# Two output blocks of the branch merge begun in four other PSUM banks, attention's half first

## The chip, the cores and the metric

The kernel runs on one core of a Trainium2 chip. The metric is the device time of one execution in microseconds. Before the change three runs took 825.71, 826.19 and 828.87 us, a median of 826.19 us.

A core works with five engines that each take their own instructions strictly in the order in which they were written down: TensorE (PE, with its weight loads shown as PEld), VectorE (DVE), ScalarE (ACT), GpSimd (POOL) and SyncE (SP), which here only issues DMAs. An instruction that waits holds up all that stand behind it on its engine. Matmuls write to PSUM, which has eight banks of 128 x 512 float32; everything else lies in SBUF.

## The reference

The program is one layer of a trunk with two parallel branches over 512 tokens (and 16 meta tokens ahead of them) of width 1024. A combined projection of the normed input feeds an RWKV-7 recurrence, a forgetting attention ("FoX") and 2 x 1024 gates. The change concerns the line that merges the two branches:

```python
u = rmsnorm(h, norm_mix[l])
proj = u @ w_in[l]
...
gates = jax.nn.sigmoid((proj[..., C_RW + C_FX:] + b_gate[l]).astype(jnp.float32))
y_rw = rwkv7_branch(feat_rw, ...)
y_fx = fox_branch(feat_fx, b_f[l], q_gain[l], k_gain[l])
merged = gates[..., :D_MODEL] * (y_rw @ w_out_rw[l]) + gates[..., D_MODEL:] * (y_fx @ w_out_fx[l])
h = h + (merged @ w_o[l]).astype(h.dtype)
z = rmsnorm(h, norm_mlp[l])
h = h + (jnp.square(jax.nn.relu(z @ w_up[l])) @ w_down[l]).astype(h.dtype)
```

## The kernel before

Activations lie transposed, features on the partitions and tokens along the free dimension. Every float32 product is made of three matmuls of rounded parts: each operand is split into a high part (a copy by ACT to the type float32r) and a low part (the difference, by DVE), and `passes` gives the pairs high-high, high-low and low-high.

**The front** (up to about 400 us) is one interleaved program. Generators ("streams": the recurrence, attention, its features, the splitting of finished branch outputs, and at the lowest rank `projections`) each yield the model time at which they can go on, and `Turns.run` always lets the stream of lowest rank that is ready write its next matmuls. That fixes the order of PE; the order of the other engines is set by a scheduler of the language, from priorities and a model of its own. The last stream to have work is `projections`: 40 blocks of 128 output columns, of which the last 16 are the gates. For each it fetches the weights (SP), splits them (L550 on ACT, L551 on DVE), multiplies (L582) and empties the bank with `gate_job` (L595 on ACT, then L596, a DMA of the gate block from tile `gt` to memory `gd`, issued on ACT's queue).

PSUM is one pool for the whole kernel: four banks with the tag "sm" for everything small, two with "pj", one "ch" and one "py". The chain of the recurrence uses "ch" and "py" while it runs; the projections use "pj", and the other two when the chain is over.

**The merge** (L1250 to L1273) follows. It makes `merged` in eight blocks `m` of 128 features. For each block the weights `wout[m]` are loaded in two halves by `load_w`: the first half (k 0 to 3) belongs to the recurrence, the second (k 4 to 7) to attention. Raw halves, high parts `whi` and low parts `wlo` have rings of four buffers each, that is two blocks. For each of the two branches the block takes a gate tile `gl` from memory (L1261), a tanh on ACT (L1262), a bank "sm" by `ppo` and 12 matmuls (4 k's of 3 passes, L1267), which DVE takes out together with the gate (L1269). POOL adds the two branches (L1271), ACT and DVE split the sum into `mhi` and `mlo` (L1272, L1273). The split branch outputs `ys[k]` are the streaming operands, k 0 to 3 of the recurrence (k 0, 1 from its first two head pairs, ready early, and k 2, 3 from the last two) and k 4 to 7 of attention. After the merge come the product with `wo` (L1298, L1329), which takes its banks from both sets, and the MLP.

A tile ring gives its oldest buffer to a new tile, so a new `whi` waits until PE has finished with the `whi` four tiles before it.

Of the kernel before, what the change touches and what calls it, by code (L numbers as in the profile page):

```python
# [147 lines left out]
class Event:  # L148
    done = False
# [40 lines left out]
def kernel(ctx, tc, ht, x, win, par, cst, gain, lora, wout, wo, wup, wdn, out, dbg=None):  # L190
    nc = tc.nc
    dbg = dbg or {}
    mm = nc.tensor.matmul
# [89 lines left out]
    ps = ctx.enter_context(tc.tile_pool(name="ps", bufs=2, space=PSUM))  # L283
    gates_d = [dr.tile([128, S], F32, name=f"gd{i}") for i in range(16)]
    ys = {}
    quarters = [[wdn[i][256 * c:256 * c + 256] for c in range(8)] for i in range(4)]

    with ExitStack() as st:
# [254 lines left out]
        def convert(job, raws):  # L543
# [9 lines left out]
                w.append((hi, lo))  # L553
            return job, w

        def projections(total):
            fetched, done = None, 0
            while done < total:
                if fetched is None:
                    yield lambda: 0.0 if jobs else math.inf  # L560
                    fetched = fetch(jobs.pop(0))
                cur = convert(*fetched)
                fetched = fetch(jobs.pop(0)) if jobs else None
                while cur is not None:
                    (_, _, _, begin, parts, ev, need), w = cur
                    nxt = convert(*fetched) if fetched else None
                    fetched = fetch(jobs.pop(0)) if jobs else None
                    if need is not None:
                        yield need
                    evac = begin()  # L570
                    for a0, a1 in parts:
                        po = None
                        n = 0
                        for k in range(KB):
                            if k % 2 == 0 or a1 - a0 > 300:
                                yield lambda f=po is None: max(ck.ready(*w[k // 4]), block_bank()[0] if f else 0.0)
                            if po is None:
                                tag = block_bank()[2]
                                po = ppj(tag)[:, :a1 - a0]
                                lent.extend([tag] * (tag != "pj"))  # L580
                            for a, b in passes(wk(w, k), U):
                                mm(po, a, b[:, k, a0:a1], start=n == 0, stop=n == 23)  # L582
                                n += 1
                        evac(po, slice(a0, a1))
                        if tag in lent:
                            lent.remove(tag)
                    ev.done = True
                    done += 1
                    cur = nxt

        def gate_job(i):
            def begin():
# [13 lines left out]
        def two(j, k):  # L606
            ys[4 * j + k] = t = kp.tile([128, 2, S], F32R, name="ys", tag=SLOTS[(4 * j + k) // 2], bufs=2)
            return t[:, 0, :], t[:, 1, :]

        def divided():  # L610
            yield chained[1]
            for k in range(2):
                split(*two(0, k), y_rw[:, k, :])
            for k in range(3):
                yield fox_done[k]
                split(*two(1, k), y_fx[:, k, :])
            yield normalised[1][1]
            for k in range(2, 4):
                split(*two(0, k), y_rw[:, k, :])

        forgot = Event()

# [102 lines left out]
        def attention():  # L725
# [3 lines left out]
            for p in range(4):  # L729
# [67 lines left out]
                def mixed():  # L797

                    yield lambda: max(ck.ready(vt, vm, pTm, *pT), banks(1))
                    py = psm("py")  # L800
                    for e, hs in enumerate(hss):
                        mm(py[hs], vm[32 * e:32 * e + 16, hs], pTm[32 * e:32 * e + 16, :], start=True, stop=False)
                    for j, at in enumerate((0, 4, 8, 7)):
                        for e, hs in enumerate(hss):
                            mm(py[hs, 128 * j:], vt[:, j, hs], pT[e][:, at:at + 4 - j, :].rearrange("p a b -> p (a b)"), start=False, stop=j == 3)  # L805
                        if j == 0:
                            yield lambda: 0.0
                    if p < 3:
                        A.copy(y_fx[:, p, :], py)
                    else:  # L810
                        yield chained[1]
                        split(*two(1, 3), py)

                pes = yield from scored(0)
                for i in range(4):
# [411 lines left out]
        turns.add(3, fox_features())  # L1227
        turns.add(4, divided())
        turns.add(8, projections(24 + 16))
        for i in range(16):  # L1230
            ask(9, B_GATE + i, gate_job(i), SEQ)
        with tc.manual_schedule(engines={mybir.EngineType.PE}):
# [16 lines left out]

    with ExitStack() as st:  # L1250
        mp = st.enter_context(tc.tile_pool(name="mp", bufs=1))
        ahead = [load_w(wout[0])]
        mhi = mp.tile([128, KB, S], F32R, name="mhi")
        mlo = mp.tile([128, KB, S], F32R, name="mlo")
        table["pin"] = None
        for m in range(KB):
            w = ahead.pop() if ahead else load_w(wout[m])
            pp = []
            for br in range(2):
                g = mp.tile([128, S], F32, name=f"gl{br}", bufs=2)  # L1260
                nc.sync.dma_start(g, gates_d[8 * br + m])  # L1261
                act(g, g, AF.Tanh, scale=0.5)  # L1262
                po = ppo()
                n = 0
                for k in range(4 * br, 4 * br + 4):
                    for a, b in passes(wk(w, k), (0, 1)):
                        mm(po, a, ys[k][:, b, :], start=n == 0, stop=n == 11)  # L1267
                        n += 1
# [347 lines left out]
```

## Time and profile before

| | |
|---|---|
| median of three runs | 826.19 us (825.71 to 828.87) |
| the profiled execution's own time | 826.71 us |
| its span | 824.9 us, so 1.8 us lie around it |
| PE busy | 808.1 us (98%) |
| DVE, ACT, POOL busy | 607.8, 452.5, 120.0 us |
| matmuls of the merge (L1267) | 192, first at 400.1 us, last at 444.7 us |
| granted TensorE clock, mean over the core | 0.998 |

The chain of waits follows the work that ended last back from the end. The table of windows gives what each engine was busy in a stretch of time, and the timeline gives the instructions of one engine with their starts, durations and, in brackets, the idle time ahead of them and what ended it. Matmuls overlap in the array, so their starts are to be compared rather than their durations. PEclk is the share of full clock that TensorE was granted.

### The profile page before, as it was taken

Reading aid. Unit: us, or ns where it says so; the run is one execution under the profiler, and the core shown is the slowest. Engines: PE = TensorE matmul, PEld = TensorE weight load, DVE = VectorE, ACT = ScalarE, POOL = GpSimd, SP = SyncE. Lnnn points to the kernel's source line nnn. Section 1 sums busy time; section 2 is a strip of 40 time slices with the busy share of each in tenths; the row PEclk is TensorE's granted clock in tenths of the full one; section 3 lists DMA queues with packets and bytes.
Section 4 is the critical chain, followed back from the end, with each engine's and each line's share of the span. In section 5 each row is a group of like instructions: output and inputs, shape, how many; then the busy total and the mean of one; then the engine's idle time right before and its main releaser. Section 6 shows DMA issues by size and latency. Waiting matters only on the chain.

```text
span 824.9 us, 15506 instructions
## 1 busy us (share of the span) xinstructions
PE 808.1 (98%) x5886; PEld 667.3 (81%) x5886; DVE 607.8 (74%) x1196; ACT 452.5 (55%) x941; POOL 120.0 (15%) x124
## 2 busy tenths in 40 slices
PE   8999999998999999999999999999999999999998
PEld 6979887876987886778788889888888888888886
DVE  6797985687779855975267655875698678867988
ACT  7767548766575457664366534664445434543452
POOL 1021000010011000000022003100740174017400
PEclk9999999999999999999999999999999999999999
DMA  7222221211211311223687404533742365236532
GB/s 240 75 71 79 69 92 56 79 40 65 79 52 54 128 46 61 90 66 116 218 289 226 159 0 151 176 82 100 225 150 87 115 221 150 77 118 208 156 107 76
DMA packets 51483, 95.88 MB, mean 116 GB/s; under 512 B 5832, under 2 KB 7240, under 8 KB 51408
## 3 DMA queue, kind: packets, MB, share of 16 engines
q1 hardware_dynamic: 47680, 86.37, 33.0%
q0 software_dynamic: 1280, 4.20, 1.7%
q10 hardware_dynamic: 2448, 4.33, 1.5%
q8 instruction: 46, 0.75, 0.4%
q14 instruction: 29, 0.24, 0.1%
HBM read 88.56 MB, written 6.31 MB: 115 GB/s over the span
## 4 chain that ended last, share of the span: by engine, by line
PE 86%; DVE 5%; ACT 5%; issue 2%; DMA 1%; POOL 0%; DVEq 0%; ACTq 0%; SPq 0%
PE pj L582 22%; PE po L1357 21%; PE po L1484 12%; PE pd L1484 5%; PE po L1267 4%; PE po L1329 3%; PE pj L394 1%; PE pd L1298 1%; PE po L1298 1%; PE psc L751 1%; PE py L805 1%; PE psr L964 1%; PE ppt L788 1%; DVE wlo L551 1%; PE pch L1115 1%
## 5 line engine op out<-in xcount | busy, mean ns | idle before, releaser
L582 PE MATMUL pj<-uhi,whi 128*128 128x264 f32 (+1 forms) x480 | 164.3, 342 | 0.0
L582 PE MATMUL pj<-uhi,wlo 128*128 128x264 f32 (+1 forms) x480 | 153.9, 321 | 1.8 <-DVE wlo L551 1.8
L582 PE MATMUL pj<-ulo,whi 128*128 128x264 f32 (+1 forms) x480 | 153.8, 320 | 0.0
L242 DVE TENSOR_TENSOR wlo<-wraw,whi 128x512 fp32r<-128x512 f32 x84 | 81.0, 973 | 36.8 <-ACT whi L242 36.8
L582 PEld LDWEIGHTS pj<-uhi,whi 128*128 128x128 f32 x480 | 90.7, 189 | 12.9 <-issue 4.4
L582 PEld LDWEIGHTS pj<-uhi,wlo 128*128 128x128 f32 x480 | 90.7, 189 | 8.8 <-DVE wlo L551 2.2
L582 PEld LDWEIGHTS pj<-ulo,whi 128*128 128x128 f32 x480 | 91.0, 190 | 6.7 <-issue 1.6
L1357 PE MATMUL po<-zhi,whi 128*128 128x512 f32 (+1 forms) x248 | 94.8, 382 | 0.0
L1357 PE MATMUL po<-zlo,whi 128*128 128x512 f32 (+1 forms) x248 | 94.8, 382 | 0.0
L1357 PE MATMUL po<-zhi,wlo 128*128 128x512 f32 (+1 forms) x248 | 94.8, 382 | 0.0
L242 ACT CAST whi<-wraw 128x512 fp32r<-128x512 f32 x84 | 51.4, 617 | 53.5 <-PE po L1357 20.3
L551 DVE TENSOR_TENSOR wlo<-wraw,whi 128x512 fp32r<-128x512 f32 x78 | 53.8, 699 | 23.5 <-ACT whi L550 22.6
L550 ACT CAST whi<-wraw 128x512 fp32r<-128x512 f32 x78 | 47.7, 617 | 42.4 <-PE pj L582 41.7
L276 ACT CAST whi<-t 128x512 fp32r<-128x512 f32 x64 | 39.9, 624 | 44.6 <-DVE wlo L276 27.2
L1406 POOL TENSOR_TENSOR t<-traw 128x512 f32<-128x512 f32 x24 | 38.4, 1622 | 173.6 <-DMA traw<-in_wdn 173.6
L1484 PE MATMUL po<-wlo,fhi 128*128 128x512 f32 (+1 forms) x164 | 63.4, 387 | 0.2
L1484 PE MATMUL po<-whi,flo 128*128 128x512 f32 (+1 forms) x164 | 62.8, 384 | 0.0
L1484 PE MATMUL po<-whi,fhi 128*128 128x512 f32 (+1 forms) x164 | 62.3, 384 | 0.0
L276 DVE TENSOR_TENSOR wlo<-t,whi 128x512 fp32r<-128x512 f32 x64 | 43.5, 689 | 24.3 <-ACT whi L276 24.0
L1373 ACT CAST fhi<-R 128x768 fp32r<-128x768 f32 (+1 forms) x32 | 30.2, 945 | 49.1 <-DVE R L1380 26.1
L1357 PEld LDWEIGHTS po<-zlo,whi 128*128 128x128 f32 x248 | 46.6, 188 | 9.1
L1357 PEld LDWEIGHTS po<-zhi,wlo 128*128 128x128 f32 x248 | 46.6, 188 | 9.0
(330 smaller groups left out, 1706.4 us busy)
## 6 DMA issues: line engine op xcount, KB each, us to landing
wraw<-in_win SPq DMA_DIRECT2D x84, 256.0 KB, 2.6
wraw<-in_wup SPq DMA_DIRECT2D x60, 256.0 KB, 3.1
wraw<-in_wdn SPq DMA_DIRECT2D x48, 256.0 KB, 2.7
traw<-in_wdn SPq DMA_DIRECT2D x48, 256.0 KB, 3.5
gd<-gt ACTq DMA_DIRECT2D x16, 256.0 KB, 2.2
wraw<-in_wout SPq DMA_DIRECT2D x16, 256.0 KB, 3.9
gl<-gd SPq DMA_DIRECT2D x16, 256.0 KB, 3.8
traw<-in_wdn POOLq DMA_DIRECT2D x16, 256.0 KB, 3.1
```

The costliest lines, as they stand in the source:

```text
L242: casts.append((A.copy(hi, raw), low.tensor_tensor(lo, raw, hi.bitcast(F32), ALU.subtract)))
L276: return A.copy(hi, x), V.tensor_tensor(lo, x, hi.bitcast(F32), ALU.subtract)
L550: after(A.copy(hi, raw), last["ACT"])
L551: low[0] = V.tensor_tensor(lo, raw, hi.bitcast(F32), ALU.subtract)
L582: mm(po, a, b[:, k, a0:a1], start=n == 0, stop=n == 23)
L1267: mm(po, a, ys[k][:, b, :], start=n == 0, stop=n == 11)
L1298: mm(pd[i], a[:, k, 128 * i:128 * i + 128], b, start=k == 0 and n == 0, stop=k == 7 and n == 2)
L1329: mm(po, a[:, k, 128 * i:128 * i + 128], b[:, k, :], start=n == 0, stop=n == 23)
L1357: mm(po[:, t0:t1], a, b[:, k, t0:t1], start=n == 0, stop=n == 23)
L1373: A.copy(fhi[:, j, a:b], R[:, a:b])
L1406: eng.tensor_tensor(t, sums[c, pair] if c in (T1, T2) else c, d, ALU.add)
L1484: mm(x[i][:, cols], a[:, k, left, 128 * rows:128 * rows + 128], c[:, cols], start=start and k == 0 and n == 0, stop=stop and k == n_pairs ...
```

## The change

A new stream `merging`, of the rank of `projections`, begins when all projections are written down. For the blocks m = 0 and 1 it takes a bank of the other set for each branch (both "pj" banks for m = 0, "ch" and "py" for m = 1) and writes into it 6 matmuls of the recurrence's half (k 0 and 1) and all 12 of attention's half (k 4 to 7). Together these are 36 matmuls. The bank and the number of matmuls done are kept in `under`. The merge loop then takes these banks over, writes the missing 6 matmuls of the recurrence's half (k 2 and 3) for each of the two blocks, and goes on with blocks 2 to 7 in the banks "sm" as before. In all eight blocks attention's half (`br` 1) now comes first, so the sum is gathered in attention's gate tile. The weights of `wout[0]` are asked for inside the front.

```diff
--- before.py
+++ after.py
@@ -283,6 +283,7 @@
     ps = ctx.enter_context(tc.tile_pool(name="ps", bufs=2, space=PSUM))
     gates_d = [dr.tile([128, S], F32, name=f"gd{i}") for i in range(16)]
     ys = {}
+    under = {}
     quarters = [[wdn[i][256 * c:256 * c + 256] for c in range(8)] for i in range(4)]
 
     with ExitStack() as st:
@@ -553,6 +554,8 @@
                 w.append((hi, lo))
             return job, w
 
+        begun, parted, projected = [], {}, Event()
+
         def projections(total):
             fetched, done = None, 0
             while done < total:
@@ -564,6 +567,8 @@
                 while cur is not None:
                     (_, _, _, begin, parts, ev, need), w = cur
                     nxt = convert(*fetched) if fetched else None
+                    if done == total - 1:
+                        begun.append(load_w(wout[0]))
                     fetched = fetch(jobs.pop(0)) if jobs else None
                     if need is not None:
                         yield need
@@ -587,6 +592,31 @@
                     ev.done = True
                     done += 1
                     cur = nxt
+            projected.done = True
+
+        def merging():
+
+            yield projected
+            for m in range(2):
+                w = begun.pop() if m == 0 else load_w(wout[m])
+                pos = []
+                for br, ks in ((0, (0, 1)), (1, (4, 5, 6, 7))):
+                    if m:
+                        yield chained[1]
+                    tag = ("pj", ("ch", "py")[br])[m]
+                    yield lambda: max(ck.ready(*w[br]), ck.ring(tag, 1, 1 if m else 2))
+                    po = ppj(tag)
+                    n = 0
+                    for k in ks:
+                        while k not in parted:
+                            yield lambda: math.inf if k not in parted else 0.0
+                        yield lambda: ck.ready(parted[k])
+                        for a, b in passes(wk(w, k), (0, 1)):
+                            mm(po, a, ys[k][:, b, :], start=n == 0, stop=n == 11)
+                            n += 1
+                    pos.append((po, n))
+                under[m] = w, pos
+            return
 
         def gate_job(i):
             def begin():
@@ -607,16 +637,21 @@
             ys[4 * j + k] = t = kp.tile([128, 2, S], F32R, name="ys", tag=SLOTS[(4 * j + k) // 2], bufs=2)
             return t[:, 0, :], t[:, 1, :]
 
+        def part(j, k, y):
+            hi, lo = two(j, k)
+            split(hi, lo, y)
+            parted[4 * j + k] = lo
+
         def divided():
             yield chained[1]
             for k in range(2):
-                split(*two(0, k), y_rw[:, k, :])
+                part(0, k, y_rw[:, k, :])
             for k in range(3):
                 yield fox_done[k]
-                split(*two(1, k), y_fx[:, k, :])
+                part(1, k, y_fx[:, k, :])
             yield normalised[1][1]
             for k in range(2, 4):
-                split(*two(0, k), y_rw[:, k, :])
+                part(0, k, y_rw[:, k, :])
 
         forgot = Event()
 
@@ -809,7 +844,7 @@
                         A.copy(y_fx[:, p, :], py)
                     else:
                         yield chained[1]
-                        split(*two(1, 3), py)
+                        part(1, 3, py)
 
                 pes = yield from scored(0)
                 for i in range(4):
@@ -1227,6 +1262,7 @@
         turns.add(3, fox_features())
         turns.add(4, divided())
         turns.add(8, projections(24 + 16))
+        turns.add(8, merging())
         for i in range(16):
             ask(9, B_GATE + i, gate_job(i), SEQ)
         with tc.manual_schedule(engines={mybir.EngineType.PE}):
@@ -1249,20 +1285,18 @@
 
     with ExitStack() as st:
         mp = st.enter_context(tc.tile_pool(name="mp", bufs=1))
-        ahead = [load_w(wout[0])]
         mhi = mp.tile([128, KB, S], F32R, name="mhi")
         mlo = mp.tile([128, KB, S], F32R, name="mlo")
         table["pin"] = None
         for m in range(KB):
-            w = ahead.pop() if ahead else load_w(wout[m])
+            w, pos = under.get(m) or (load_w(wout[m]), [])
             pp = []
-            for br in range(2):
+            for br in (1, 0):
                 g = mp.tile([128, S], F32, name=f"gl{br}", bufs=2)
                 nc.sync.dma_start(g, gates_d[8 * br + m])
                 act(g, g, AF.Tanh, scale=0.5)
-                po = ppo()
-                n = 0
-                for k in range(4 * br, 4 * br + 4):
+                po, n = pos[br] if pos else (ppo(), 0)
+                for k in range(4 * br + n // 3, 4 * br + 4):
                     for a, b in passes(wk(w, k), (0, 1)):
                         mm(po, a, ys[k][:, b, :], start=n == 0, stop=n == 11)
                         n += 1
```

The number of matmuls stays the same, and up to the last projection all engines have the same rows in the same order. In the rows below the names are tiles with their numbers: `whi_5490` and `whi_5496` (with `wlo_5491`, `wlo_5497`) are the two halves of the weights of block m = 2 in both programs, the recurrence's and attention's; line numbers of the changed program are 30 to 35 higher.

ScalarE, from the last gate's bank on, before:

```order
L595 ACTIVATE gt_5374<-pj_5349,pr_64 128x512
L596 DMA gd15_95<-gt_5374 128x512
L242 CAST whi_5490<-wraw_5488 128x512
L242 CAST whi_5496<-wraw_5494 128x512
L1262 ACT_TABLE_LOAD
L1262 ACTIVATE gl0_5402<-gl0_5402 128x512
L1262 ACTIVATE gl1_5419<-gl1_5419 128x512
L1262 ACTIVATE gl0_5451<-gl0_5451 128x512
L1262 ACTIVATE gl1_5468<-gl1_5468 128x512
L242 CAST whi_5539<-wraw_5537 128x512
L1272 ACTIVATE mhi_5400<-gl0_5402 128x512
```

ScalarE at the same place in the changed program:

```order
L625 ACTIVATE gt_5386<-pj_5361,pr_64 128x512
L626 DMA gd15_95<-gt_5386 128x512
L242 CAST whi_5490<-wraw_5488 128x512
L1297 ACT_TABLE_LOAD
L1297 ACTIVATE gl1_5454<-gl1_5454 128x512
L1297 ACTIVATE gl0_5458<-gl0_5458 128x512
L1297 ACTIVATE gl1_5471<-gl1_5471 128x512
L1297 ACTIVATE gl0_5475<-gl0_5475 128x512
L242 CAST whi_5496<-wraw_5494 128x512
L242 CAST whi_5539<-wraw_5537 128x512
L1306 ACTIVATE mhi_5452<-gl1_5454 128x512
```

`whi_5490` still stands ahead of the load of the tanh table and the four tanhs of the gate tiles of m = 0 and 1, `whi_5496` has moved behind all four. `whi_5490` takes the buffer of the first half of m = 0 (`whi_5351` in the changed program, `whi_5390` before), `whi_5496` that of its second half.

VectorE, from the low parts of the same weights on, before:

```order
L242 TENSOR_TENSOR wlo_5491<-wraw_5488,whi_5490 128x512
L242 TENSOR_TENSOR wlo_5497<-wraw_5494,whi_5496 128x512
L1269 SCALAR_TENSOR_TENSOR gl0_5402<-gl0_5402,po_5405 128x512
L1269 SCALAR_TENSOR_TENSOR gl1_5419<-gl1_5419,po_5422 128x512
L1269 SCALAR_TENSOR_TENSOR gl0_5451<-gl0_5451,po_5454 128x512
L242 TENSOR_TENSOR wlo_5540<-wraw_5537,whi_5539 128x512
L1273 SCALAR_TENSOR_TENSOR mlo_5401<-gl0_5402,mhi_5400 128x512
```

VectorE at the same place in the changed program:

```order
L242 TENSOR_TENSOR wlo_5491<-wraw_5488,whi_5490 128x512
L1303 SCALAR_TENSOR_TENSOR gl1_5454<-gl1_5454,pj_5396 128x512
L1303 SCALAR_TENSOR_TENSOR gl0_5458<-gl0_5458,pj_5389 128x512
L1303 SCALAR_TENSOR_TENSOR gl1_5471<-gl1_5471,pj_5428 128x512
L242 TENSOR_TENSOR wlo_5497<-wraw_5494,whi_5496 128x512
L1303 SCALAR_TENSOR_TENSOR gl0_5475<-gl0_5475,pj_5421 128x512
L1307 SCALAR_TENSOR_TENSOR mlo_5453<-gl1_5454,mhi_5452 128x512
L242 TENSOR_TENSOR wlo_5540<-wraw_5537,whi_5539 128x512
```

`wlo_5497` stands behind three gates' products now, where it stood ahead of all of them.

TensorE in the changed program, from the last matmuls of m = 0 on (rows with x2 are two matmuls):

```order
L1301 MATMUL pj_5389<-ys_5298,whi_5351 128x512 x2
L1301 MATMUL pj_5389<-ys_5298,wlo_5352 128x512
L1301 MATMUL pj_5421<-ys_5295,whi_5411 128x512 x2
L1301 MATMUL pj_5421<-ys_5295,wlo_5412 128x512
L1301 MATMUL pj_5421<-ys_5298,whi_5411 128x512 x2
L1301 MATMUL pj_5421<-ys_5298,wlo_5412 128x512
L1301 MATMUL po_5503<-ys_5124,whi_5496 128x512 x2
L1301 MATMUL po_5520<-ys_5118,whi_5490 128x512 x2
L1301 MATMUL po_5503<-ys_5124,wlo_5497 128x512
```

TensorE before, around the same 49th matmul after the last projection:

```order
L1267 MATMUL po_5471<-ys_5115,whi_5447 128x512 x2
L1267 MATMUL po_5471<-ys_5115,wlo_5448 128x512
L1267 MATMUL po_5503<-ys_5118,whi_5490 128x512 x2
L1267 MATMUL po_5503<-ys_5118,wlo_5491 128x512
L1267 MATMUL po_5503<-ys_5121,whi_5490 128x512 x2
```

The last use of m = 0's first half is now in the 14th pair of rows (matmuls 40 to 42 after the last projection); before it was in the fourth (matmuls 10 to 12). The 49th matmul reads `whi_5496` and a bank "sm" that nobody holds; before, it read `whi_5490` and a bank that the first gate's product has to free.

## The prediction

> **What bounds the kernel now.** I read the page first: PE is busy for nearly the whole span and carries most of the chain of waits. So a PE instruction that starts later moves the end, and idle time elsewhere does not.
>
> ```profile
> span 824.9 us, 15506 instructions
> PE 808.1 (98%) x5886; PEld 667.3 (81%) x5886; DVE 607.8 (74%) x1196; ACT 452.5 (55%) x941; POOL 120.0 (15%) x124
> PE 86%; DVE 5%; ACT 5%; issue 2%; DMA 1%; POOL 0%; DVEq 0%; ACTq 0%; SPq 0%
> ```
>
> Next came the windows around the place of the change (columns: stretch, length, busy time of each engine, PEclk, DMA share, GB/s).
>
> ```profile
> 390.00:400.00 10.00, 10.00 (x46) 8.29 (x45) 4.19 (x7) 4.07 (x7) 0.00 (x0) 1.00 0.43 139
> 400.00:445.00 45.00, 43.97 (x194) 36.08 (x194) 25.71 (x39) 25.12 (x42) 9.55 (x7) 1.00 0.81 262
> 445.00:480.00 35.00, 35.00 (x160) 29.07 (x159) 21.21 (x37) 18.56 (x39) 2.09 (x2) 1.00 0.46 150
> ```
>
> The projections' last stretch and the stage behind the merge have no idle PE at all. The merge has 1.0 us. That bounds what the change can win: the matmuls are the same, and 36 of them only change their bank. PE's timeline shows where the microsecond lies.
>
> ```profile
> 400.06 0.62 PE L1267 MATMUL po<-ys,whi 128*128 128x512 f32 x2
> 408.90 0.62 PE L1267 MATMUL po<-ys,whi 128*128 128x512 f32 x2
> 410.72 0.39 PE L1267 MATMUL po<-ys,wlo 128*128 128x512 f32 x1
> 412.13 0.73 PE L1267 MATMUL po<-ys,whi 128*128 128x512 f32 x2 [1.03 <-DVE gl L1269]
> 444.90 0.39 PE L1298 MATMUL po<-whi,mhi 128*128 128x512 f32 x1
> ```
>
> Matmuls 1 and 48 of the merge start at 400.06 and 410.72, so one takes 10.66 / 47 = 0.227 us. The 49th could start at 410.95 and starts at 412.13, 1.18 us late: it needs a fifth bank "sm", and the first is freed by DVE only after the gate has come. The chain says why the gate is late.
>
> ```profile
> 401.28 5.43 DMA gd<-gt
> 406.79 2.59 DMA gl<-gd
> 412.13 32.93 PE po L1267 x144
> ```
>
> The last gate's store from `gt` lands at 406.71, only then are the gate tiles fetched, and the first lands at 409.38. Between 412.13 and 444.90 the remaining 144 matmuls run without a gap.
>
> **The change part by part.** *Banks.* Blocks 0 and 1 use the other four banks, so matmul 49 finds an empty "sm" bank. This removes the wait on DVE: 1.18 us, if nothing else holds matmul 49. The bank of m = 0's attention half is the last gate's; ACT empties it by 401.24 (row of L595 below), and that half's first matmul is the 7th, at 400.06 + 6 x 0.227 = 401.42. It fits by 0.2 us; I count 0, and at most 0.1.
>
> *Weights of m = 2.* Here the new wait enters. These are ACT's and DVE's rows before.
>
> ```profile
> 400.56 0.68 ACT L595 ACTIVATE gt<-pj,pr 128x512 f32<-128x512 f32 x1
> 402.75 0.62 ACT L242 CAST whi<-wraw 128x512 fp32r<-128x512 f32 x1 [1.51 <-PE po L1267]
> 405.48 0.62 ACT L242 CAST whi<-wraw 128x512 fp32r<-128x512 f32 x1 [2.10 <-PE po L1267]
> 409.43 1.28 ACT L1262 ACT_TABLE_LOAD   x1 [3.33 <-DMA gl<-gd]
> 410.73 1.15 ACT L1262 ACTIVATE gl<-gl 128x512 f32<-128x512 f32 x2
> 412.32 1.34 ACT L1262 ACTIVATE gl<-gl 128x512 f32<-128x512 f32 x2 [0.45 <-DMA gl<-gd]
> 413.56 0.60 ACT L242 CAST whi<-wraw 128x512 fp32r<-128x512 f32 x1
> 411.39 1.28 DVE L1269 SCALAR_TENSOR_TENSOR gl<-gl,po 128x512 f32<-128x512 f32 x2 [4.57 <-ACT gl L1262]
> ```
>
> The casts at 402.75 and 405.48 are m = 2's two halves, both done long before matmul 49. By the changed order the recurrence's half waits for matmul 41 (last user of the `whi` buffer), and attention's half, which matmul 49 now reads, stands behind the table load and four tanhs. Step by step:
>
> - Matmul 11 starts at 400.06 + 10 x 0.227 = 402.33, and the cast that it released started at 402.75, 0.42 later. Matmul 41 starts at 400.06 + 40 x 0.227 = 409.13, so the first cast runs from 409.55 to 410.17.
> - The table load could start before at 409.43, with the first gate; now 410.19, to 411.47. The two conditions lie 0.7 us apart, so the gate's DMA hardly counts any more.
> - Four tanhs at a pitch of 1.15 - 0.63 = 0.52 from 411.49 on: starts 411.49, 412.01, 412.53, 413.05. Before, the third started when its DMA landed (412.32) and the fourth by 413.03, so no landing binds.
> - Attention's cast from 413.57 to 414.19. From DVE's first product (411.39 + 0.68) to matmul 49 there were 0.06 us, so matmul 49 starts at 414.25.
>
> That is 414.25 - 412.13 = 2.1 us later than before; the gap grows from 1.2 to 3.3 us. Its low part on DVE ends near 414.9; four matmuls with high parts are ahead of it, 414.25 to some 415.2, so it adds nothing. The bounds: 2.1 if the gate lands as in this execution; up to 3.3 where it lands early, since before would then not have waited at all while the new chain hangs on matmul 41. A later landing delays both alike.
>
> *What is queued behind.* Block 3's halves are cast after the same tanhs and one `mhi`, which waits for POOL:
>
> ```profile
> 412.81 1.29 POOL L1271 TENSOR_TENSOR gl<-gl,gl 128x512 f32<-128x512 f32 x1 [152.62 <-DMA wraw<-in_wout]
> 416.17 1.66 POOL L1271 TENSOR_TENSOR gl<-gl,gl 128x512 f32<-128x512 f32 x1 [2.07 <-DVE gl L1269]
> gl<-gd SPq DMA_DIRECT2D x16, 256.0 KB, 3.8
> 408.64 0.85 SPq L239 DMA_DIRECT2D wraw<-in_wout  x2
> ```
>
> With DVE's second product done at 413.4, POOL ends by 415.1, `mhi` by 415.8, the cast by 416.3, and after `mlo` and two low parts DVE is done at 417.7. PE needs them at 414.25 + 24 x 0.227 = 419.7: 2 us to spare. SP is now blocked until 410.9 by block 4's raw weights (408.64 before) and again until 414.9. The gate for the first bank that returns is issued near 416.5, lands at 420.3 by the 3.8 us of the row, and its product is out by 423; the bank is needed at 425.2. These cost 0, and at most 1 us if DMAs land 3 us late. Turning the branches round is symmetrical.
>
> *The clock.* A longer gap can cost more than itself. Once in this execution the granted clock fell: after PE had waited 1.52 us.
>
> ```profile
> 201.93 1.17 PE L751 MATMUL psc<-ka,qa 64*128 64x256 f32 x4 [1.52 <-DVE nm L762]
> 202.00:203.00 1.00, 1.00 (x4) 0.52 (x4) 0.85 (x5) 0.35 (x1) 0.00 (x0) 1.00 0.00 0
> 203.00:204.00 1.00, 1.00 (x17) 0.85 (x16) 0.94 (x3) 0.00 (x0) 0.00 (x0) 0.58 0.00 0
> 204.00:205.00 1.00, 1.00 (x9) 0.88 (x6) 1.00 (x4) 0.66 (x2) 0.14 (x1) 0.50 0.00 0
> 205.00:206.00 1.00, 1.00 (x7) 1.00 (x6) 1.00 (x4) 0.97 (x3) 0.14 (x1) 0.50 0.00 0
> 206.00:207.00 1.00, 1.00 (x8) 1.00 (x8) 0.81 (x6) 0.71 (x2) 0.00 (x0) 0.71 0.38 125
> 50.74 0.50 PE L582 MATMUL pj<-uhi,wlo 128*128 128x512 f32 x1 [1.80 <-DVE wlo L551]
> 50.70:55.00 4.30, 4.26 (x39) 3.33 (x40) 4.23 (x10) 2.02 (x5) 0.14 (x1) 1.00 0.56 182
> 205.03 0.42 PE L582 MATMUL pj<-uhi,whi 128*128 128x264 f32 x1
> 205.25 0.42 PE L582 MATMUL pj<-ulo,whi 128*128 128x264 f32 x1
> 207.07 0.28 PE L582 MATMUL pj<-uhi,wlo 128*128 128x264 f32 x1
> 207.19 0.28 PE L582 MATMUL pj<-uhi,whi 128*128 128x264 f32 x1
> ```
>
> The clock fell not at once but at 203.2, and stood at 0.50 for (0.42 + 0.5 + 0.5 + 0.29) / 0.5 = 3.4 us; equal matmuls came every 0.22 us instead of 0.12. One such drop therefore costs 3.4 x (1 - 0.12 / 0.22) = 1.5 us, or 1.7 by the clock itself; I take 1.6. A wait of 1.80 us among full matmuls did not bring it. [...] I take one drop: +1.6 us, with 0 and 3.2 (two drops) as bounds.
>
> [...]
>
> *Sum*, against the profiled execution's 826.71 us: -1.18 for the bank wait, +3.30 for the weights, +1.6 for the clock, 830.4. That execution lies 0.5 us above the median of the three runs, so the forecast for the median is 826.19 + 3.7 = **829.9 us**, 0.45% above before.
>
> **The rivals.**
>
> *The gap without the drop.* The same +2.1 us, clock at 1.00 as behind the gaps at 50.74 and 412.13: 828.3 us. For it speaks that two gaps above 1 us among full matmuls left no drop; against it that 3.1 us is 1.7 times the longest that was harmless here. [...]
>
> [...]
>
> *The faster end.* The idle banks do what they could: attention's cast is done before 410.95, matmul 49 follows 48, and 826.19 - 1.18 = 825.0 us. It needs ACT to reach that cast 3.3 us before the order lets it; break-even is a cast done by 412.07. The raw half is there in time, but ACT takes nothing out of order in any row here.
>
> **How the numbers follow.** One drop 0.56, no drop 0.21, two drops or an early gate 0.16, faster end 0.05, and 0.02 for something unseen. A measurement of this kernel tells about 0.5% (4.1 us, so 822.1 and 830.3 us) from no change. The forecast lies just inside. I give its part beyond the upper bound 0.14 of its 0.56, and two drops 0.13: slower 0.28. No case but an unseen one is faster by 4.1 us: 0.02. Same: 0.70. The range, 827.8 to 831.5 us, holds no drop at its lower and two drops at its upper end and leaves out the faster end and extremes.
>
> **What would show it.** In the changed kernel's timeline PE should run 48 matmuls from 400.06, then wait some 3.3 us before the first matmul of block 2, put down to ACT's `whi` (no longer to DVE's `gl`). ACT's cast should stand at 409.5, the table load right behind, attention's cast at 413.6. PEclk near 0.5 for 3.4 us, starting within 3.4 us of the gap's end, shows the clock term; the product with `wo` should start near 448.6 instead of 444.90. I am wrong if that wait ends before 412.1, or if a second wait of PE follows at blocks 3 to 5.

## The result, and the profile after

Measured again side by side in 14 executions each, the kernel before takes 827.37 us and the changed kernel 828.97 us in the median; the ratio is 1.0026, with a 95% interval of 1.0017 to 1.0036. By that ratio the change costs some 2.2 us (the two medians lie 1.6 us apart). This is inside the 0.5% that the prediction counts as no change, and inside its range (827.8 to 831.5 us, forecast 829.9). The difference is smaller than the forecast 3.7 us, though, and some steps of the reasoning were false.

The page of the changed kernel's profiled execution (828.07 us by its own time) has the same shape as before: PE is busy for 98% of the span and makes up 85% of the chain of waits.

```profile
span 826.3 us, 15501 instructions
PE 809.1 (98%) x5886; PEld 668.0 (81%) x5886; DVE 606.5 (73%) x1196; ACT 453.0 (55%) x941; POOL 119.8 (15%) x124
PE 85%; DVE 5%; ACT 5%; issue 2%; DMA 1%; SPq 1%; POOL 0%; DVEq 0%; ACTq 0%
```

The windows of the changed kernel around the merge (same columns as before) show 1.52 us of idle PE where 1.03 stood, and the clock at 1.00 throughout.

```profile
400.00:445.00 45.00, 43.48 (x192) 35.62 (x191) 25.97 (x39) 25.07 (x42) 9.55 (x7) 1.00 0.80 264
445.00:480.00 35.00, 35.00 (x160) 29.06 (x160) 20.51 (x35) 17.26 (x35) 2.08 (x2) 1.00 0.46 150
414.00:417.00 3.00, 3.00 (x15) 2.47 (x14) 3.00 (x4) 1.36 (x4) 1.67 (x1) 1.00 0.91 268
```

PE's timeline of the changed kernel (start, duration, operation, and in brackets the idle time before it with what ended it): the merge starts at 401.06, as the whole execution stands 1.0 us later by then. The 48th matmul starts at 411.74, the 49th at 413.65.

```profile
401.06 0.61 PE L615 MATMUL pj<-ys,whi 128*128 128x512 f32 x2
411.74 0.39 PE L1301 MATMUL pj<-ys,wlo 128*128 128x512 f32 x1
413.65 1.20 PE L1301 MATMUL po<-ys,whi 128*128 128x512 f32 x4 [1.52 <-ACT whi L242]
446.42 0.39 PE L1332 MATMUL po<-whi,mhi 128*128 128x512 f32 x1
```

The product with `wo` starts 446.42 - 401.06 = 45.36 us after the merge; before it was 444.90 - 400.06 = 44.84. The bank is no longer waited for, ACT's cast is. ACT's timeline of the changed kernel shows the order that the prediction read from the program, but not its times:

```profile
405.14 0.62 ACT L242 CAST whi<-wraw 128x512 fp32r<-128x512 f32 x1 [2.89 <-PE pj L615]
409.22 1.28 ACT L1297 ACT_TABLE_LOAD   x1 [3.46 <-DMA gl<-gd]
410.52 2.57 ACT L1297 ACTIVATE gl<-gl 128x512 f32<-128x512 f32 x4
413.00 1.12 ACT L242 CAST whi<-wraw 128x512 fp32r<-128x512 f32 x2
```

The first cast of m = 2 runs at 405.14, which is 4.08 us after the merge's start and not 9.5. So it holds nothing up: the table load waits for the gate's DMA, as before. Only the second cast, attention's, stands behind table load and tanhs, and matmul 49 starts 0.65 us after that cast's start. The chain of waits of the changed kernel shows one thing more. The DMA in it is the fetch of a gate tile that SP issued last of four, and it ends at 412.44, just ahead of the fourth tanh:

```profile
407.01 5.43 DMA gl<-gd
412.46 0.02 ACT gl L1297
413.00 0.61 ACT whi L242
413.65 32.93 PE po L1301 x144
```

So here the cast waits not only for the first gate's landing but for that of all four. In the kernel before, matmul 49 needed only the first gate's product.

### The profile page after: what moved, and what is told of

Its sections match the earlier page's. It is cut to its first block, busy times and chain, and to the rows that moved or that the text cites. A ratio compares the mean times of both kernels' runs of the same rounds, so it can differ in the third digit from the quotient of the medians.

```text
span 826.3 us, 15501 instructions
## 1 busy us (share of the span) xinstructions
PE 809.1 (98%) x5886; PEld 668.0 (81%) x5886; DVE 606.5 (73%) x1196; ACT 453.0 (55%) x941; POOL 119.8 (15%) x124
## 4 chain that ended last, share of the span: by engine, by line
PE 85%; DVE 5%; ACT 5%; issue 2%; DMA 1%; SPq 1%; POOL 0%; DVEq 0%; ACTq 0%
PE pj L587 22%; PE po L1391 21%; PE po L1518 12%; PE pd L1518 5%; PE po L1301 4%; PE po L1363 3%; PE pj L395 1%; PE pd L1332 1%; PE po L1332 1%; PE psc L786 1%; PE py L840 1%; PE psr L999 1%; PE ppt L823 1%; DVE wlo L552 1%; PE pch L1150 1%
## 5 line engine op out<-in xcount | busy, mean ns | idle before, releaser
L1391 PEld LDWEIGHTS po<-zhi,whi 128*128 128x128 f32 x248 | 46.6, 188 | 9.0
```

Source lines behind the costliest of these rows:

```text
L1391: mm(po[:, t0:t1], a, b[:, k, t0:t1], start=n == 0, stop=n == 23)
```

## The experiments

Each kernel ran beside the kernel before, on the same chip. The table gives the ratio to it with its 95% interval, the mean time, and how that mean splits. **Half clock** is the mean number of stretches of 3.413 us in which TensorE had half its clock, counted in lengths of the drop in the profile before (203.17 to 206.58); **rest** is the time less 1.71 us, half a stretch, for each of them. The line of the kernel before joins its executions beside the two sets of experiments (29 and 35), that of the changed kernel the 14 of the result and the 12 of after_again. Errors are standard errors of the mean.

The number of stretches is read from an execution's granted clock, of which one stretch takes 1.71 of some 826 us, that is 0.002: 0.998 or 0.997 is counted as one stretch, 0.996 or 0.995 as two, 0.994 or 0.993 as three, 0.992 or 0.991 as four, and 0.999 or more as none. This agrees with the one drop in the profile before (0.998) and the three in d_look2 (near 51, 205 and 417 us; 0.993). What lies between two such numbers is taken for a piece at the very end of the span. In after_again (0.995) the clock stood at 0.50 once more from 827.40 to 828.60, when the last matmul had long started (its row, then a window behind it):

```profile
824.65 0.28 PE L1518 MATMUL po<-whi,flo 128*128 128x256 f32 x1
827.40:828.60 1.20, 0.00 (x0) 0.00 (x0) 0.00 (x0) 0.00 (x0) 0.00 (x0) 0.50 0.00 0
```

By this reading that piece costs no time: the executions of the kernel before with 0.995 take 827.64 us in the mean, those with 0.996 827.67.

| kernel (label) | ratio | executions | mean us | half clock | rest |
|---|---|---|---|---|---|
| before | | 64 | 827.05 ± 0.12 | 1.58 ± 0.07 | 824.35 ± 0.07 |
| changed (the result and after_again) | 1.0026 [1.0013, 1.0039] | 26 | 829.24 ± 0.27 | 1.73 ± 0.12 | 826.28 ± 0.13 |
| a_casts_first | 0.9998 [0.9990, 1.0007] | 11 | 826.91 ± 0.21 | 1.55 ± 0.16 | 824.27 ± 0.26 |
| g_attention_weights_first | 0.9995 [0.9985, 1.0004] | 12 | 826.64 ± 0.28 | 1.42 ± 0.15 | 824.22 ± 0.12 |
| d_before_casts_late | 1.0045 [1.0029, 1.0060] | 6 | 830.82 ± 0.65 | 2.50 ± 0.34 | 826.54 ± 0.25 |
| b_attention_first | 1.0009 [0.9997, 1.0021] | 11 | 827.50 ± 0.35 | 1.36 ± 0.20 | 825.17 ± 0.31 |
| c_recurrence_first | 1.0030 [1.0017, 1.0043] | 12 | 829.71 ± 0.50 | 2.00 ± 0.28 | 826.29 ± 0.11 |
| e_before_gates_free | 0.9995 [0.9987, 1.0003] | 12 | 826.80 ± 0.26 | 1.67 ± 0.14 | 823.95 ± 0.04 |
| f_after_gates_free | 0.9998 [0.9987, 1.0009] | 12 | 827.19 ± 0.35 | 1.42 ± 0.15 | 824.76 ± 0.17 |

The ratio in the changed kernel's line is after_again's. Its mean excess over the kernel before, 2.19 us, is 1.92 ± 0.15 us of rest and 0.26 ± 0.23 us of clock. (The kernel before's own executions with one and two stretches differ by 1.40 us and not 1.71; priced so, the excess of rest would be 1.98.)

### The casts put back ahead of the tanhs: a_casts_first

The changed kernel with added dependencies: the four tanhs of m = 0 and 1 come behind both casts of m = 2 on ACT, and their four gate products behind both low parts of m = 2 on DVE. (Here and below, `...` marks code left out.)

```diff
+        held = [], []
...
+            if m == 2:
+                for cast in casts[-2:]:
+                    for late, part_ in zip(held, cast):
+                        for ins in late:
+                            after(ins, part_)
...
-                act(g, g, AF.Tanh, scale=0.5)
+                held[0].append(act(g, g, AF.Tanh, scale=0.5))
...
-                V.scalar_tensor_tensor(g, g, 1.0, po, ALU.add, ALU.mult)
+                held[1].append(V.scalar_tensor_tensor(g, g, 1.0, po, ALU.add, ALU.mult))
```

> The changed kernel with one thing put back: ACT must cast both halves of block 2's weights before the four tanhs of blocks 0 and 1, and DVE must make their low parts before the four gates' products. Theory (the wait of matmul 49 is ACT's order: gate landing, table load, four tanhs, then the cast): the wait of 1.52 us on ACT's whi at matmul 49 goes to 0 to 0.2 us, and the kernel gains about 2 us on the changed one; a smaller wait of up to 1 us may come at block 3, whose casts then stand behind the same tanhs. That is 0 to 1 us faster than before. Rival (the other banks or the order of the branches cost by themselves): matmul 49 no longer waits, but the time stays 1.5 to 2 us above before. In the cast of attention's half I expect a start at the release by matmul 41, some 9.5 us after the first matmul of the merge, since the other buffer that comes free earlier goes to the recurrence's half.

The ratio falls from 1.0026 to 0.9998, the rest from 826.28 to 824.27. The waits of PE in its merge and ACT's timeline:

```profile
PE po L1307 <- DVE wlo L242: 1.0, 1, 1.0
PE po L1307 <- ACT whi L242: 0.2, 1, 0.2
```

```profile
404.64 0.62 ACT L242 CAST whi<-wraw 128x512 fp32r<-128x512 f32 x1 [2.90 <-PE pj L615]
408.72 0.62 ACT L242 CAST whi<-wraw 128x512 fp32r<-128x512 f32 x1 [3.46 <-PE pj L615]
409.36 1.28 ACT L1303 ACT_TABLE_LOAD   x1
```

No wait stands at matmul 49 any more. The loss goes when the casts and their low parts stand ahead again; the begun banks and attention's half first, both still in this kernel, cost nothing that shows here. The wait of 1.0 us that it does have is a new one, at 440.81 in the last block. The times of the casts show more. The merge starts at 400.56 here, so they run 4.08 and 8.16 us after it, earlier than the 9.5 us of a release by matmul 41. Matmuls start every 0.227 us and a cast follows its release by 0.42: (4.08 - 0.42) / 0.227 is 16 matmuls, so matmul 17 released the first, and (8.16 - 0.42) / 0.227 is 34, so matmul 35 the second. By the order of the changed kernel, 17 and 35 are the last readers of the high parts of the *attention* halves of m = 0 and m = 1. So in this program the buffers go to new tiles in the order in which they are set free, not in the order in which they were taken. The sentence ahead of the prediction that a ring gives its oldest buffer to a new tile is wrong, and so is the one that `whi_5490` takes the buffer of the first half of m = 0.

### Attention's weights first: g_attention_weights_first

The changed kernel, which loads and casts attention's half ahead of the recurrence's from m = 2 on, so that the early cast is the one that matmul 49 reads.

```diff
-    def load_w(src, low=(V, V)):
+    def load_w(src, low=(V, V), order_=(0, 1)):
-        return [load_h(src[:, 512 * j:512 * j + 512], low[j], "w", (4, 4, 4)) for j in range(2)]
+        return [load_h(src[:, 512 * j:512 * j + 512], low[j], "w", (4, 4, 4)) for j in order_][::order_[1] * 2 - 1]
...
-            w, pos = under.get(m) or (load_w(wout[m]), [])
+            w, pos = under.get(m) or (load_w(wout[m], order_=(1, 0)), [])
```

> The changed kernel with one thing altered: for blocks 2 to 7 attention's half of the weights is loaded and cast ahead of the recurrence's. The half that goes ahead of the tanhs is then the one that matmul 49 reads. Theory: no wait at matmul 49; the other half is needed 2.7 us later, is cast about 4.5 us after the landing and its low part is ready at 5.2 us, that is 13.3 to 14.5 us after the first matmul of the merge where PE comes at 13.6 to 14.1, so a wait of 0 to 0.9 us at matmuls 61 to 63; 1 to 2 us faster than the changed kernel, within 1 us of before. Rival (the wait does not come from the place of this cast): the wait of 1.5 us or more at matmul 49 stays.

PE runs through the merge without a wait. In its chain of waits the matmuls behind the begun banks follow each other to the end, and in PE's timeline the 49th (413.06) comes 0.22 us after the 48th:

```profile
413.23 32.69 PE po L1301 x144
```

```profile
412.84 0.39 PE L1301 MATMUL pj<-ys,wlo 128*128 128x512 f32 x1
413.06 0.62 PE L1301 MATMUL po<-ys,whi 128*128 128x512 f32 x2
```

It is 2.6 us faster than the changed kernel in the mean, and by 0.9995 [0.9985, 1.0004] not to be told from the kernel before. This is the change with its fault taken out. Its rest lies 0.14 ± 0.14 us below before's, so a free bank is worth little by itself.

### The fault alone, in the kernel before: d_before_casts_late

The kernel before, with both casts of m = 2 made to follow the four tanhs; banks and order of the branches as they were.

```diff
+        held = []
...
+            if m == 2:
+                for hi_, lo_ in casts[-2:]:
+                    for th in held:
+                        after(hi_, th)
...
-                act(g, g, AF.Tanh, scale=0.5)
+                held.append(act(g, g, AF.Tanh, scale=0.5))
```

> The kernel before, its banks and its order of branches untouched, but both casts of block 2's weights put behind the four tanhs of blocks 0 and 1 on ACT. Theory: this alone costs what the change costs or more: matmul 49 starts about 4.5 us after the first gate lands instead of 2.75 us, and matmul 51 waits some 0.5 us more for the low part on DVE; 2.0 to 2.6 us slower by the waits, and up to 1.6 us more in executions in which the granted clock falls behind the longer gap (mean granted clock 0.995 or 0.996 instead of 0.998). Rival (the cast's place does not matter, the bank's product is late anyway): less than 0.7 us slower than before.

Its waits of PE in the merge:

```profile
PE po L1272 <- ACT whi L242: 1.7, 1, 1.7
PE po L1272 <- DVE wlo L242: 0.2, 1, 0.2
```

The rest rises by 2.19 ± 0.26 us, with none of the change's other parts. The position of the casts (here of both) is enough to make the loss, as a_casts_first and g_attention_weights_first show that it is needed for it.

### The order of the branches: b_attention_first and c_recurrence_first

The one is the kernel before with attention's half first, the other the changed kernel with the recurrence's half first again.

```diff
-            for br in range(2):
+            for br in (1, 0):
```

> The kernel before with attention's half first in the merge loop and nothing else, all banks as before. Theory: the order of the branches is symmetrical, so matmul 49 waits for DVE's first gate product as before, about 1.0 us, and the time is that of before within 0.5 us. Rival (attention first costs by itself): 1 us or more slower than before.

```diff
-            for br in (1, 0):
+            for br in range(2):
```

> The changed kernel with the recurrence's half first again in the merge loop; the banks of blocks 0 and 1 are begun as in the changed one. Matmul 49 then reads the half that ACT still casts ahead of the tanhs. Theory: no wait at matmul 49. Attention's half is needed 12 matmuls (2.7 us) later; its cast ends about 4.5 us after the gate lands, but DVE's order puts its low part behind four gate products and one mlo, about 6.9 us after the landing, so a wait on DVE's wlo of 1 to 2 us comes at matmul 63. Time 0 to 1 us above before, at or a little below the changed one. Rival (attention first is what costs): as fast as before or 1 us faster, with no wait of PE in the merge.

```profile
PE po L1267 <- DVE wlo L242: 0.7, 1, 0.7
```

```profile
418.86 0.80 PE L1301 MATMUL po<-ys,wlo 128*128 128x512 f32 x1 [2.74 <-DVE wlo L242]
```

The first row is b_attention_first's only wait in the merge, late in it (439.70). The expected wait of 1.0 us at matmul 49 is not there: the first gate landed 8.37 us after the merge's start, earlier than the 9.37 of the profile before, and matmul 49 is 0.18 us late. Attention first alone costs 0.8 ± 0.3 us of rest; in the whole time it is 0.5 us slower in the mean, the edge of what was expected, and does not stand out from the noise. The second row is c_recurrence_first's: turning the branches back does not help. Matmul 49 has its weights early now, but the cast of attention's half still stands behind the tanhs, its low part behind DVE's four products and a `mlo`, and PE stops a dozen matmuls later, for 2.7 us, longer than the expected 1 to 2. The kernel was expected 0 to 1 us above before and is 2.7 us above it in the mean, 1.9 us of that in the rest. The wait moves to the first reader of the late half.

### The gates' landing: e_before_gates_free and f_after_gates_free

Both put the gate tiles of m = 0 and 1 into memory that is free earlier, so that their fetch need not wait for the last gate's store. The one is the kernel before, the other the changed kernel.

```diff
+        gl = yp.tile([128, 4, S], F32, name="gl", tag="y_fx")
...
-                g = mp.tile([128, S], F32, name=f"gl{br}", bufs=2)
+                g = gl[:, 2 * br + m, :] if m < 2 else mp.tile([128, S], F32, name=f"gl{br}", bufs=2)
```

> The kernel before with the gate tiles of blocks 0 and 1 put into the finished attention output's memory (tag y_fx), so that their DMAs need not wait until the front's memory is given back, that is for the last gate's store. The tanh table and four tanhs then stand in the front. Theory (the first gate's landing is what holds the fifth bank): no wait of PE at matmul 49; 1.0 to 1.5 us faster than before, less what a later wait takes back (block 7's weights were about 1.0 us late where the merge ran without the first wait). Rival (the banks or DVE are late anyway): a wait of 1 us stays at matmul 49 and the time is that of before.

> The changed kernel with the same free memory for the gate tiles of blocks 0 and 1. The cast of attention's half for matmul 49 then stands behind two tanhs of block 2's gates, which still wait for the front's memory, without the table load and two of the four tanhs. Theory: the cast ends some 1.8 us after that landing, at 9.9 to 11.1 us after the first matmul of the merge where PE comes at 10.9 us, so the wait shrinks to 0 to 0.3 us and its low part on DVE to at most 0.7 us; 1.5 to 2.5 us faster than the changed kernel, as fast as the same edit on the kernel before. Rival (the begun banks cost by themselves): it stays 1 us or more behind the same edit on the kernel before.

The kernel before loses its bank wait by this: its chain shows the merge's 192 matmuls in one piece.

```profile
402.32 43.52 PE po L1268 x192
```

It gains 0.40 ± 0.08 us of rest, though, and not the 1.18 us of the profiled execution, on which the expectation was built. In the mean execution the bank wait was small, then. The changed kernel wins back 1.5 us of rest by the same edit. It was expected to become as fast as e_before_gates_free and does not: its rest stays 0.81 ± 0.17 us above. In its profile the one wait left in the merge is 0.8 us, near 441, in the last block; b_attention_first has one of 0.7 us at this place and a_casts_first one of 1.0. All three take attention's half first. That this order costs the time there is likely but not shown: g_attention_weights_first has it too and does not wait.

### Further profiles of the changed kernel: after_again, changed_look2, changed_look3, changed_look4, d_look2

The changed kernel four times more, and d_before_casts_late once more; no edits. They are to show how far the wait varies, and when the clock falls.

> The changed kernel once more, unaltered, beside the same runs of before as the next three. Theory from the first four runs: 1.0 to 2.5 us slower than before; of that about 1.5 us by the wait of matmul 49 and the rest by executions whose mean granted clock is 0.995 or 0.996 instead of 0.998. Rival (the clock is chance and not of the change): as many executions at 0.998 as the kernel before has, and the difference is 1.5 us among executions of the same clock and over all alike.

> The changed kernel itself, to see where the clock falls. [...] Matmul 49 should stand 4.4 us behind the start of the table load. [...]

> [...]

> [...]

> The kernel before with both casts of block 2 held behind the four tanhs, once more: in its six executions the clock was never above 0.996, the largest loss of all. [...]

Five profiles of the changed kernel are there with the first. The landing of the gate is read as the start of the table load, and counted from the merge's start; the lateness of matmul 49 is the idle time in its row plus 0.16 us, since the row before counts as busy for 0.39 us and the next matmul could follow after 0.227. The last column is an estimate that applies the chain of the kernel before to the same landing: there matmul 49 stood 412.13 - 409.43 = 2.70 us behind the table load, and could have started 10.89 us after the merge's start. (b_attention_first bears the rule out: at its landing of 8.37 it gives 0.18 us, and 0.18 was measured.)

| profile | landing | idle before matmul 49 | late by | before would be late by |
|---|---|---|---|---|
| the result's | 8.16 | 1.52 | 1.68 | 0.00 |
| after_again | 9.35 | 2.90 | 3.06 | 1.16 |
| changed_look2 | 8.25 | 1.23 | 1.39 | 0.06 |
| changed_look3 | 8.72 | 1.69 | 1.85 | 0.53 |
| changed_look4 | 8.50 | 1.68 | 1.84 | 0.31 |
| mean | 8.60 | 1.80 | 1.96 | 0.41 |

The difference of the means, 1.55 us, is the larger part of the 1.92 ± 0.15 us by which the rest rose; five profiles are few, and where the other 0.4 us lie is not shown. The 0.41 us agree with the 0.40 that e_before_gates_free won. The landing of the profiled execution before (409.43 - 400.06 = 9.37) was a late one. One cause is the last gate's store, which took 3.48 us in changed_look2 and 5.39 in after_again:

```profile
401.86 3.48 DMA gd<-gt
```

```profile
403.25 5.39 DMA gd<-gt
```

The first landing alone does not set the wait. Matmul 49 was expected 4.4 us behind the start of the table load; it stands 4.04 us behind it in changed_look2 and changed_look3, but 4.43, 4.62 and 4.26 in the result's profile, after_again and changed_look4, where the chain of waits goes through the fetch of the fourth gate. d_look2 shows it most clearly. Its first gate landed 7.89 us after the merge's start, earlier than in any row above, and yet matmul 49 waited for 2.52 us, longer than the 1.69 us of changed_look3 at a landing of 8.72: the fourth tanh waited for its own gate, whose fetch took 6.29 us (first row after_again, second d_look2).

```profile
414.82 0.63 ACT L1297 ACTIVATE gl<-gl 128x512 f32<-128x512 f32 x1 [0.46 <-DMA gl<-gd]
```

```profile
414.80 0.63 ACT L1267 ACTIVATE gl<-gl 128x512 f32<-128x512 f32 x1 [1.01 <-DMA gl<-gd]
```

*The clock.* Near 50 us each of the 14 profiles has a wait of PE of 1.80 us (1.81 in changed_look4). In six of them (after_again, e_before_gates_free, f_after_gates_free, g_attention_weights_first, changed_look4 and d_look2) full matmuls behind it came every 0.43 us in place of 0.23; in the other eight they did not. The waits in the merge went with the clock as follows:

| profile | wait of PE in the merge, us | clock behind it |
|---|---|---|
| changed_look2 | 1.23 | no matmuls at 0.43 us |
| the result's | 1.52 | 1.00 |
| changed_look4 | 1.68 | no matmuls at 0.43 us |
| changed_look3 | 1.69 | no matmuls at 0.43 us |
| d_before_casts_late | 1.74 | 1.00 |
| d_look2 | 2.52 | 0.50 from 416.72 on, for 3.4 us |
| c_recurrence_first | 2.74 | 0.50 from 418.10 on, for 6.8 us |
| after_again | 2.90 | 1.00 |

The length of the wait does not sort these cases, and what else does is not shown. The pair that tells most is after_again and d_look2. The first waits longer, and PEclk stays at 1.00 (its PE row, then its windows).

```profile
416.01 1.21 PE L1301 MATMUL po<-ys,whi 128*128 128x512 f32 x4 [2.90 <-ACT whi L242]
```

```profile
413.00:416.00 3.00, 0.10 (x1) 0.00 (x0) 1.90 (x4) 2.54 (x6) 1.23 (x1) 1.00 0.94 326
416.00:418.00 2.00, 1.99 (x9) 1.62 (x10) 2.00 (x4) 1.52 (x3) 0.68 (x2) 1.00 0.85 307
418.00:420.00 2.00, 2.00 (x10) 1.68 (x9) 2.00 (x2) 0.76 (x2) 1.03 (x1) 1.00 0.94 263
```

In d_look2 the wait is shorter, and the clock is half from 416.72 to 420.12:

```profile
415.98 0.73 PE L1272 MATMUL po<-ys,whi 128*128 128x512 f32 x2 [2.52 <-ACT whi L242]
```

```profile
416.00:417.00 1.00, 1.00 (x3) 0.57 (x4) 1.00 (x2) 1.00 (x3) 0.00 (x0) 0.86 0.71 287
417.00:420.00 3.00, 3.00 (x8) 2.35 (x8) 3.00 (x4) 1.40 (x3) 1.66 (x1) 0.50 0.67 232
420.00:421.00 1.00, 1.00 (x6) 0.83 (x5) 1.00 (x3) 0.82 (x2) 0.00 (x0) 0.94 0.46 104
```

## Why the prediction held, and which step failed

**The removed bank wait** went as the step said: in none of the five profiles does PE wait for DVE's `gl`. But its price, 1.18 us, was that of an execution with a late gate; in the mean it is about 0.4 us by the estimate above and the gain of e_before_gates_free.

**The new wait** is the one forecast, ACT's cast of attention's half behind table load and four tanhs; a_casts_first and d_before_casts_late show it from both sides. The step that failed is the one before it, that the early cast hangs on matmul 41: "Matmul 41 starts at [...] 409.13, so the first cast runs from 409.55". The first cast was released by matmul 17 and done 3.5 us ahead of the table load (405.14 + 0.62 to 409.22). It follows that "the gate's DMA hardly counts any more" is wrong as well: the chain starts with the landing, as it did before. The landings of the later gates were put at nothing ("so no landing binds"); in three of the five profiles the fourth one does bind. At a landing like the one it reckoned with (after_again) the two kernels differ by 3.06 - 1.16 = 1.9 us. That the forecast's 2.1 us are near it is luck: it holds some 0.8 us for a table load held up by the first cast, which did not happen, and nothing for the fourth gate, which cost some 0.6 there (4.62 us behind the table load against the forecast's 414.25 - 410.19 = 4.06). "A later landing delays both alike" holds for the first gate only. Where the gate lands early, the prediction held that the loss would grow to 3.3 us, as a bound; it shrinks to some 1.3 to 1.7, as the new wait shrinks with it. The term was 2.1 and measured 1.92 ± 0.15.

**Nothing behind it** was right: the changed kernel's profile has this one wait of PE in the merge and no second one.

```profile
PE po L1301 <- ACT whi L242: 1.5, 1, 1.5
```

**The clock** was mis-sized. The term of 1.6 us stood on two estimates. That a drop costs 1.6 us is about right: of the 64 executions of the kernel before, 25 have one stretch of half clock, mean 826.26 us, and 38 have two, mean 827.66, which is 1.40 us. That one drop comes behind the gap, put at 3.1 us (414.25 less 411.11, the end of matmul 48's row), no run of the changed kernel shows: in its five profiles, with waits of 1.23 to 2.90 us, none followed the merge's wait, and over its 26 executions the term is 0.26 ± 0.23 us, not clear of nothing. By the granted clock alone the difference would be 0.64 us, but by the reading above the larger part of that is the piece at the end of the span. In d_before_casts_late there are 0.9 ± 0.35 more stretches than before, and d_look2, with a wait of 2.52 us, shows one behind the merge's wait.

**The sum** was 3.7 us and measured 2.2 us: 0.2 us too much for the weights, 1.3 for the clock. So the clock is the term that failed in size, and the weights' term is right in size with a wrong step in it. The forecast of 829.9 us came nearer to 828.97 than that by luck, since the three runs shown of the kernel before had a median of 826.19, and later ones 827.37. By its parts, what came is the rival without a drop (2.1 us and 828.3), which had a chance of 0.21.

**The rivals.** Two drops behind the merge's wait, which the upper bound of 3.2 us holds, did not come in the five profiles of the changed kernel; in c_recurrence_first 6.8 us of half clock followed a wait of 2.74 us a dozen matmuls further on. The faster end needed the cast ahead of the tanhs, as it said, but its 825.0 us were too hopeful even then: g_attention_weights_first has it so, and comes out 0.4 us below before in the mean, not 1.2.

## What to carry to other kernels

Freeing the resource that a wait names is worth what the next condition leaves, so before taking it, look what else the waiting instruction reads and what stands ahead of that work on its in-order engine; here a bank wait of 0.4 us in the mean gave way to one of 2.0 us (both estimated from five profiles) for a cast behind four tanhs, which wait for four DMAs and not for one. Let the operand that is used first also be cast first: exchanging the two halves took the loss away without another change. And price a wait that hangs on a DMA from several executions; the one profiled here had it at 1.18 us, the mean at 0.4.

## What the runs showed of the hardware

The same store of 256 KB from `gt` took 3.4 us (d_before_casts_late) to 5.6 us (c_recurrence_first), and the fetch of a gate tile of the same size up to 6.3 us (d_look2); with them the wait of PE in the changed kernel varied between 1.2 and 2.9 us. The granted clock fell to half behind some waits of PE and not behind others: a wait of 1.80 us near 50 us was followed by half clock in 6 of 14 profiles, one of 2.52 us in the merge too (d_look2), one of 2.90 us not (after_again). Behind a wait of 1.52 us near 200 us, among smaller matmuls, the rows up to 206 us show the slower rate in 13 of 14 profiles (in after_again not by then); in the profile before, PEclk was 0.50 there from 203.17 to 206.58. The executions of the kernel before differ by 1.4 us with one stretch of half clock more or less (826.26 and 827.66 us). The windows of after_again show its drop behind the wait near 50 us:

```profile
51.00:53.00 2.00, 1.76 (x7) 1.38 (x7) 2.00 (x6) 0.51 (x1) 0.14 (x1) 0.87 0.37 116
53.00:55.00 2.00, 2.00 (x27) 1.18 (x25) 1.54 (x5) 0.65 (x2) 0.00 (x0) 0.50 0.71 245
```
